# A hybrid decoder layer on one core: sums on DVE, stores from ACT's queue, a bank for the last piece, later turns

## The chip, the cores and the metric

The kernel runs on one core of a Trainium2 chip. The metric is the device time of one launch in microseconds. The core has the tensor engine (TensorE, PE in the profile; its weight loads are PEld), the vector engine (DVE), the scalar engine (ACT), GpSimd (POOL) and SyncE (SP), which here only issues DMAs. Each engine works through its own instructions in order; semaphores hold an instruction until what it reads or overwrites is ready, and everything behind it on that engine waits with it.

## The reference

One layer (DEPTH 1) on 1024 tokens of width 1024, float32. A token mixer (sliding-window attention with sinks beside a gated DeltaNet, merged by gates, one output projection `mixed`), then a squared-ReLU MLP, both post-norm with adaLN modulation:

```
x  = layer_norm(ALPHA * x + (1 + gt1) * mixed, ln1_g, ln1_b)
u2 = x * (1 + sc2) + sh2
h  = square(relu(u2 @ w_ff1 + b_ff1))                  # 1024 x 4096
x  = layer_norm(ALPHA * x + (1 + gt2) * (h @ w_ff2 + b_ff2), ln2_g, ln2_b)
```

The change lies wholly behind the mixer's projections: in `mixed` (the product with `w_out`) and the first layer norm, in FF1 (`u2 @ w_ff1`) and in FF2 (`h @ w_ff2`).

## The kernel before

**Precision.** Each float32 operand is split into a high and a low part (`split_s`: ACT copies the high part, DVE subtracts to give the low one some matmuls later), and each product is three matmuls: high x high, high x low, low x high.

**Order of the work.** The order on TensorE, DVE and ACT is written out by hand. `count[0]` counts the matmuls issued; `at(p, f, ...)` puts a piece of work at matmul number p, `after(n, ...)` n matmuls from now, and before each matmul the loop emits what is due (`run_events`). The number of an event is a place in the engines' program order, not a time: an engine that is late does the work later, in that order. SP and POOL are not held to it; their order is made by a planner with a model of costs, and then is as fixed as the others'.

**The mix stage (from E0 to F0).** Four stretches s of the product with w_out, over token tiles t of 128. When a tile's second half is there, `mix_done` gates it, adds the residual, takes bn statistics, has ACT take a square root (L1392) and DVE normalise (`norm`, L1394 to L1397), and stores the tile. `u2_done` then plans the tile's turn: TensorE transposes it (`u2_turn`, L1407, into PSUM tag b, two buffers), ACT copies it out with scale and bias (L1410), and it is split into U11, U21, U22 and the sums T1 to T4. Tiles 6 and 7 come last.

**FF1 (from F0 to G0).** A Strassen-like scheme: the 1024 x 4096 product is cut in block pairs i = 0 to 15, and each pair is seven products m of 12 matmuls (L1866), 84 in all. For i below EARLY = 5 the products 1 and 2 of all pairs come first, and the rest follow in periods of 60 matmuls; from i = 5 a pair is 84 in a row. `PROD` says which weights a product takes: a and g are the first weight tile before and after sums, b the second after a sum, d their difference x. So each pair needs four additions on 128 x 512 (`f_sums`: x and the second tile; `f_sums2`: the first tile), after its two weight tiles are loaded (`f_load`, tile fraw, two pairs deep) and ahead of the splits `f_beta`, `f_gamma`, `f_delta`. x is in one buffer. For i = 1 and i of 5 and more the sums are on DVE, for i = 2, 3 and 4 on POOL.

ACT copies the result of a begun bank out with its bias (`part`, L1585), which frees the bank for the next product that adds into it; `full` adds a second product on DVE and `square` does relu and square; `last_block` does the same for the last product; `block_done` stores a finished block (c = 0, 2, 3) to the DRAM tensor hf_d with `put`, on SP's queue. `again` reads one block back, `h_sums` and `h_sums2` form and store the sums of blocks that FF2 takes.

Meanwhile POOL makes FF2's weight sums: `t_load` loads a pair of w_ff2 tiles (wx), `t_make` does four subtractions and stores them to wt_d. The first 13 of 16 rounds fall in FF1.

**FF2 (from G0).** Seven products m in the order 1, 2, 6, 5, 3, 7, 4, each of eight steps s of 24 matmuls over four PSUM banks (L1907). `s_load` loads a step's two operands, `s_split` splits operand j = 0 and 1; the first steps are placed from p15, the start of pair 15. In the last product the last four steps are done tile by tile, and the last tile in two pieces of 256 columns, both in its one bank; `gated` adds each piece up, `norm2` does the second layer norm and stores it.

The line numbers are those of the profile: L1407 and L1410 are in `u2_turn`, L1435 in `sub`, L1543 in `add_`, L215 and L216 in `split_s`.

Of the kernel before, what the change touches and what calls it, by code (L numbers as in the profile page):

```python
# [9 lines left out]
F32 = mybir.dt.float32  # L10
F32R = mybir.dt.float32r
BF16 = mybir.dt.bfloat16
AF = mybir.ActivationFunctionType
ALU = mybir.AluOpType
# [3 lines left out]
P = 128  # L18
D = 1024
S = 1024  # L20
KT = D // P
NT = S // P
HALF = 512
# [11 lines left out]
def hybrid_layer_kernel(ctx: ExitStack, tc: tile.TileContext,  # L35
                        x, c, w_ada, b_ada, w_in, conv_w, a_log, dt_bias, sinks, dn_norm_w,
                        w_oa, w_ob, w_out, ln1_g, ln1_b, w_ff1, b_ff1, w_ff2, b_ff2,
                        ln2_g, ln2_b, out, dbg=None):
    nc = tc.nc
    x, c, out = x[0], c[0], out[0]  # L40
# [6 lines left out]
    V, A, G, T = nc.vector, nc.scalar, nc.gpsimd, nc.tensor  # L47

    const = ctx.enter_context(tc.tile_pool(name="const", bufs=1))
    wp = ctx.enter_context(tc.tile_pool(name="wp", bufs=4))  # L50
# [4 lines left out]
    def psum(tag, bufs, name=None):  # L55
        return ps.tile([P, HALF], F32, tag=tag, bufs=bufs, name=name or tag)
# [23 lines left out]
    hf_d = dram.tile([7, D_FF // (2 * P), P, HALF], F32, name="hf_d")  # L80
# [21 lines left out]
    eps_ln = const.tile([P, 1], F32, name="eps_ln")  # L102
# [92 lines left out]
    events, count, order = [], [0], [0]  # L195

    def at(p, f, *args):
        order[0] += 1
        heapq.heappush(events, (p, order[0], f, args))

    def after(n, f, *args):
        at(count[0] + n, f, *args)
# [275 lines left out]
    for step in ('t0 s0 o00 o01 w0 w1 d4 t1 s1 v203 o10 v235 o11 v256 m0 t2 p2 s2 v304 o20 v346 o21 m1 t3 p3 s3 v404 o30 v446 o31 m2 '  # L478
                 't4 p4 s4 v504 o40 v546 o41 m3 t5 p5 s5 r0 v604 o50 v646 o51 m4 t6 p6 s6 v704 o60 v746 o61 m5 t7 p7 s7 o70 o71 m6').split():
        f, k = step[0], int(step[1])  # L480
# [900 lines left out]
    def mix_done(second, q, t, pt):  # L1381
        r = rs[t]
        rq = r[:, halves[q]]
        tm = pe.tile([P, HALF], F32, tag="t", name="tm", bufs=6)
        V.tensor_tensor(out=tm, in0=pt, in1=gt1[:, halves[q]], op=ALU.mult)
        V.scalar_tensor_tensor(out=rq, in0=rq, scalar=ALPHA, in1=tm, op0=ALU.mult, op1=ALU.add)
        V.bn_stats(out=parts[:, t, q, :], in_=rq)
        if not second:
            return
        st = pe.tile([P, 4], F32, tag="st", name="st", bufs=3)  # L1390
        V.bn_aggr(out=st[:, 0:2], in_=parts[:, t].rearrange("p q s -> p (q s)"))
        after(1, lambda: A.activation(out=st[:, 2:3], in_=st[:, 1:2], func=AF.Sqrt, bias=eps_ln))  # L1392

        def norm():  # L1394
            V.reciprocal(out=st[:, 3:4], in_=st[:, 2:3])
            V.tensor_scalar(out=r, in0=r, scalar1=st[:, 0:1], scalar2=st[:, 3:4], op0=ALU.subtract, op1=ALU.mult)
            nc.gpsimd.dma_start(out=res_d[t], in_=r)  # L1397
        after(4, norm)

    def u2_turn(j, us, ks):  # L1400

# [72 lines left out]
    wt, bank = [], 0  # L1474
# [28 lines left out]
    for s in range(4):  # L1503
        q, t0 = (0, 1, 1, 0)[s], 4 * (s // 2)
        if s != 2:
            del wt[:]
        groups = [[0, 1], [2, 3]] if s < 2 else [[4, 5], [6, 7]] if s == 2 else [[4, 5], [6], [7]]
        for ts in groups:
            pts = []
            for t in ts:  # L1510
                tag = ("mm", "a", "mm", "c", "mm", "a")[bank % 6]
                bank += 1
                pts.append(psum(tag, {"mm": 3, "a": 2, "c": 1}[tag]))
            for c in range(4):
                if len(wt) == c:
                    run_events(count[0])
                    wt.append(ready.pop(0))
                for pt, t in zip(pts, ts):
                    mix_mm(pt, slice(t * P, (t + 1) * P), c)
            for pt, t in zip(pts, ts):  # L1520
                at(max(count[0] + (14 if s == 2 and t > 5 else 1), E0 + 28), mix_done, s % 2 == 1, q, t, pt)
                if s % 2 == 1:
                    at(count[0] + 1, u2_done, t, count[0] + (26 if t == 7 else 34))

# [15 lines left out]
    def add_(E, out, a, b):  # L1542
        E.tensor_tensor(out=out, in0=a, in1=b, op=ALU.add)  # L1543
# [33 lines left out]
        f = i + NPAIR * (c // 2)  # L1577
        return bf1[:, f:f + 1]

    def put(m, i, t):  # L1580
        nc.sync.dma_start(out=hf_d[m - 1, i], in_=t)

    def part(i, c, pt):

# [1 line left out]

    def block_done(i, c):
        if c != 1:
            put({0: 1, 2: 2, 3: 4}[c], i, tls[i, c])

    def square(i, c):
        t = tls[i, c]
# [58 lines left out]
    for i in range(1, NPAIR):  # L1651
        if i < EARLY:
            b = pos[i, 5]
            E = V if i == 1 else G
            at(b - 70, f_load, i)
            at(b - (26 if i == 1 else 46), f_sums, i, E)
            at(b - (25 if i == 1 else 44), f_sums2, i, E)
            at(b - 17, f_beta, i)
            at(b - 3, f_gamma, i)
            at(b + 10, f_delta, i)  # L1660
        else:
            b = pos[i, 1]
            at(b - 104, f_load, i)
            at(b - (34 if i == EARLY else 76), f_alpha, i)
            at(b - (28 if i == EARLY else 66), f_sums, i, V)
            at(b - (27 if i == EARLY else 60), f_sums2, i, V)
            at(b + (8 if i == EARLY else -44), f_gamma, i)
            at(b + (26 if i == EARLY else -9), f_beta, i)
            at(max(b - (0 if i == EARLY else 22), pos[i - 1, 7] + 13), f_delta, i)
# [155 lines left out]
    for s in range(7 * NS):  # L1825
        p = G0 + 24 * s
        at((p15 + 14, p15 + 26, p15 + 62, p15 + 64)[s] if s < 4 else p - 96 - 28, s_load, s)
        for j in range(2):
            if s < 2:
                q = p15 + (40, 64)[s] + 8 * j  # L1830
            elif s >= 6 * NS:
                q = p - (94 if s > 6 * NS else 70) + 10 * j
            else:
                q = p - 46 + 10 * j
            at(q, s_split, s, j)
# [52 lines left out]
    def take(dst, pt, copy):  # L1888
        if copy:
            A.activation(out=dst, in_=pt, func=AF.Copy)  # L1890
        else:
            add_(V, dst, dst, pt)

    for n, m in enumerate(ORDER):
        ab = "C" if m in (2, 5, 3) else "A"
        begin = m in (1, 2, 5)
# [2 lines left out]
                         for tag in (("mm", "mm", "a", "c") if ab == "A" else ("mm", "a", "b", "b"))]  # L1899
        bank = chain[ab]  # L1900

        def step(s, f, t, lo=0, up=HALF):
            for x_ in range(3):
                run_events(count[0])
                (ah_, al_), (bh, bl) = stp[s, 0], stp[s, 1]
                a, b = ((ah_, bh), (ah_, bl), (al_, bh))[x_]
                T.matmul(bank[t][:, lo:up], lhsT=a[:, f, t * P:(t + 1) * P], rhs=b[:, f, lo:up],  # L1907
                         start=begin and s % NS == 0 and f == 0 and x_ == 0,
                         stop=s % NS == NS - 1 and f == 1 and x_ == 2, skip_group_check=True)
                count[0] += 1  # L1910

        def steps(ss, tile_first):
            if tile_first:
# [15 lines left out]
        if m == 4:  # L1929
            for _ in steps(range(s0 + 1, s0 + NS - LAST), False):  # L1930
                pass
            for t in range(4):

                cuts = [0, HALF] if t < 3 else [0, HALF // 2, HALF]
                for i, (lo, up) in enumerate(zip(cuts, cuts[1:])):
                    for s in range(s0 + NS - LAST, s0 + NS):
                        for f in range(2):
                            step(s, f, t, lo, up)
                    after(1, gated, 4 + t, lo, up, 1 + i, bank[t][:, lo:up])
                after(1, norm2, 4 + t, [(HALF, D), (0, HALF)], 1 + len(cuts) - 1)  # L1940
            break
        for _ in steps(range(s0 + 1, s0 + NS - 1), False):
# [43 lines left out]
```

## Time and profile before

| what | us |
|---|---|
| runs: median, lowest, highest of 3 | 1913.79, 1913.71, 1917.88 |
| profiled execution: time | 1912.24 |
| its span | 1910.5 |
| TensorE busy in the span | 1833.2 |
| DVE busy | 1289.8 |
| ACT busy | 976.0 |
| POOL busy | 422.6 |

The profile is of one execution. Times in it count from the span's start. A group of instructions is written "line engine operation out<-in", with the idle time of the engine before it and what ended that idle time in brackets. In the list of waits the three numbers are the total, the number of waits and the longest. In the stretches of time the columns are, for each engine, busy time and number of instructions, then the granted clock of TensorE, the share of time in which the DMA engines were busy, and GB/s. A matmul of 128 x 512 is shown as about 0.39 us long while one starts each 0.227 us, since matmuls overlap. The letter behind PE is the PSUM tag that it writes.

### The profile page before, as it was taken

What the parts mean: (1) busy time and instruction counts of PE and PEld (TensorE: products, weight loads), DVE (VectorE), ACT (ScalarE), POOL (GpSimd) and SP (SyncE); (2) the same over time, 40 slices, a digit from 0 to 9 for tenths busy, and PEclk for the clock granted to TensorE, in tenths of its full rate; (3) what the DMA queues carried; (4) which work ended last, traced back from release to release, by engine and by line L of the source; (5) the groups of instructions that cost most, each with busy time, mean ns of one, the idle gap of its engine ahead of it and who ended that gap; (6) DMA issues with size and microseconds to landing.
All of it is one profiled execution on the core that took longest, in us unless ns stands there. A gap on an engine that the chain in (4) does not pass through costs nothing.

```text
span 1910.5 us, 26004 instructions
## 1 busy us (share of the span) xinstructions
PE 1833.2 (96%) x9137; PEld 1513.2 (79%) x9137; DVE 1289.8 (68%) x2395; ACT 976.0 (51%) x2105; POOL 422.6 (22%) x521
## 2 busy tenths in 40 slices
PE   7999999999999999999999999995899999999997
PEld 5977788788887878888888888774687887888886
DVE  7678598998856666666644446872677556676696
ACT  3689666666654445544634223562454554434441
POOL 7333233443331000000001100035644002300000
PEclk7999999999999999999999999997999999999998
DMA  9655632232257444554337444465888449955571
GB/s 257 181 189 198 209 95 82 59 97 79 72 195 218 149 137 144 156 152 142 112 132 264 141 136 154 144 230 201 287 274 279 143 153 394 362 192 176 198 243 44
DMA packets 261644, 337.72 MB, mean 177 GB/s; under 512 B 25237, under 2 KB 170342, under 8 KB 261258
## 3 DMA queue, kind: packets, MB, share of 16 engines
q1 hardware_dynamic: 230954, 227.62, 37.7%
q0 software_dynamic: 30560, 108.44, 16.6%
q8 instruction: 72, 1.18, 0.2%
q14 instruction: 58, 0.48, 0.1%
HBM read 231.40 MB, written 102.51 MB: 175 GB/s over the span
## 4 chain that ended last, share of the span: by engine, by line
PE 73%; DVE 10%; DMA 4%; ACT 4%; issue 3%; POOL 2%; SPq 0%; POOLq 0%; ACTq 0%; DVEq 0%
PE mm L248 32%; PE mm L1907 6%; PE mm L1866 5%; PE a L1907 4%; PE b L1907 3%; PE b L1866 3%; PE c L1907 2%; DVE wl L216 2%; PE c L909 2%; PE a L1866 1%; DMA wx<-in_w_ff_dram 1%; PE mm L1498 1%; POOL wx L1435 1%; PE mm L188 1%; PE mm L187 1%
## 5 line engine op out<-in xcount | busy, mean ns | idle before, releaser
L248 PE MATMUL mm<-uh,wl 128*128 128x512 f32 x800 | 331.4, 414 | 0.0
L248 PE MATMUL mm<-ul,wh 128*128 128x512 f32 x800 | 320.8, 401 | 0.0
L248 PE MATMUL mm<-uh,wh 128*128 128x512 f32 x800 | 317.3, 397 | 0.0
L216 DVE TENSOR_TENSOR sp<-sraw,sp 128x1024 fp32r<-128x1024 f32 x112 | 137.8, 1264 | 75.3 <-ACT sp L215 75.3
L215 ACT ACTIVATE sp<-sraw 128x1024 fp32r<-128x1024 f32 x112 | 112.7, 1053 | 125.0 <-PE b L1907 65.4
L248 PEld LDWEIGHTS mm<-ul,wh 128*128 128x128 f32 x800 | 150.6, 188 | 26.5 <-issue 0.2
L248 PEld LDWEIGHTS mm<-uh,wl 128*128 128x128 f32 x800 | 151.4, 189 | 22.8 <-issue 3.9
L248 PEld LDWEIGHTS mm<-uh,wh 128*128 128x128 f32 x800 | 151.3, 189 | 21.2 <-issue 0.2
L1907 PE MATMUL mm<-sp 128*128 128x512 f32 x528 | 136.1, 389 | 0.0
L216 DVE TENSOR_TENSOR wl<-fraw,wh 128x1024 fp32r<-128x1024 f32 x43 | 62.4, 1453 | 80.6 <-ACT wh L215 80.3
L1907 PEld LDWEIGHTS mm<-sp 128*128 128x128 f32 x528 | 99.1, 188 | 20.5
L1435 POOL TENSOR_TENSOR wx<-wx 128x512 f32<-128x512 f32 x64 | 94.9, 1482 | 75.3 <-DMA wx<-in_w_ff_dram 73.8
L216 DVE TENSOR_TENSOR wl<-wr,wh 128x1024 fp32r<-128x1024 f32 x81 | 98.7, 1219 | 8.1 <-ACT wh L215 8.1
L215 ACT ACTIVATE wh<-wr 128x1024 fp32r<-128x1024 f32 x81 | 84.9, 1049 | 21.6 <-PE c L1498 12.3
L1907 PE MATMUL a<-sp 128*128 128x512 f32 x336 | 92.6, 389 | 0.0
L1169 ACT ACTIVATE vn<-a,brk 128x128 f32<-128x128 f32 x64 | 23.5, 367 | 108.1 <-PE a L1167 107.2
L1593 ACT ACTIVATE t<-t 128x512 f32<-128x512 f32 x48 | 30.1, 627 | 93.1 <-DVE t L1543 93.1
L853 POOL TENSOR_TENSOR sm<-sm 128x256 f32<-128x256 f32 x56 | 55.6, 993 | 97.7 <-ACT sm L849 65.0
L842 DVE CUSTOM_DVE_ANT_0 nscore<-a,amask,nsink 128x256 f32<-128x256 f32 (+1 forms) x128 | 54.6, 464 | 33.5 <-PE a L835 32.7
L1907 PEld LDWEIGHTS a<-sp 128*128 128x128 f32 x336 | 63.1, 188 | 13.1
L1907 PE MATMUL b<-sp 128*128 128x512 f32 x288 | 72.8, 389 | 0.0
L215 ACT ACTIVATE wh<-fraw 128x1024 fp32r<-128x1024 f32 x43 | 45.2, 1053 | 40.7 <-POOL fraw L1543 33.3
(520 smaller groups left out, 4746.9 us busy)
## 6 DMA issues: line engine op xcount, KB each, us to landing
wr<-in_w_in_dram SPq DMA_DIRECT2D x60, 512.0 KB, 3.6
sraw<-hf_d SPq DMA_DIRECT2D x56, 512.0 KB, 4.4
fraw<-in_w_ff_dram SPq DMA_DIRECT2D x32, 512.0 KB, 4.5
hf_d<-t SPq DMA_DIRECT2D x64, 256.0 KB, 4.5
wx<-in_w_ff_dram POOLq DMA_DIRECT2D x32, 512.0 KB, 6.4
wt_d<-wx POOLq DMA_DIRECT2D x32, 512.0 KB, 3.7
sraw<-wt_d SPq DMA_DIRECT2D x32, 512.0 KB, 4.6
sraw<-in_w_ff_dram SPq DMA_DIRECT2D x24, 512.0 KB, 5.7
```

The lines of the kernel that those rows point to most:

```text
L187: T.matmul(t, lhsT=wh[:, k, :], rhs=xl[k][:, sl], start=False, stop=False)
L215: A.activation(out=hi, in_=src, func=AF.Copy)
L216: after(lag, lambda: V.tensor_tensor(out=lo, in0=src, in1=hi.bitcast(F32), op=ALU.subtract))
L248: T.matmul(ts[half], lhsT=w[:, k, :], rhs=xx[k][:, sl], start=k == 0 and m == 0, stop=k == KT - 1 and m == 2)
L842: V.tensor_tensor_reduce(out=ns[:, i, 1:1 + W], in0=sc[:, i * 2 * P:i * 2 * P + W], in1=amask[:, mo:mo + W], scale=-1.0, scalar=nsink[:, 2 ...
L853: G.tensor_tensor(out=sm[:, :, 1 + P:1 + 2 * P], in0=sm[:, :, 1:1 + P], in1=sm[:, :, 1 + P:1 + 2 * P], op=ALU.add)
L909: T.matmul(av[:, 0:256], lhsT=vt[:, b, :], rhs=p_[:, m, :], start=p_ is full and m == 0, stop=p_ is prods[-1][1] and m == 1)
L1169: after(1, lambda: A.activation(out=vn, in_=Wp[:, 0:P], func=AF.Copy, scale=brk[:, n, h:h + 1]))
L1435: E.tensor_tensor(out=out, in0=a, in1=b, op=ALU.subtract)
L1593: A.activation(out=t, in_=t, func=AF.Relu)
L1866: T.matmul(pt, lhsT=a[:, k0 + k, :], rhs=b[k], start=begin and k == 0 and x_ == 0, stop=k == 3 and x_ == 2, skip_group_check=True)
L1907: T.matmul(bank[t][:, lo:up], lhsT=a[:, f, t * P:(t + 1) * P], rhs=b[:, f, lo:up], start=begin and s % NS == 0 and f == 0 and x_ == 0, sto ...
```

## The change

- The sums of i = 2, 3, 4 go from POOL to DVE, at 40 and 36 matmuls ahead of product 5 instead of 46 and 44.
- `block_done` stores the finished blocks from ACT's queue. The other users of `put` stay on SP.
- For tiles 6 and 7 the square root comes 20 and 12 matmuls after `mix_done` instead of 1, the normalisation three behind it, and the turn at 46 and 40 matmuls instead of 34 and 26.
- The splits of FF2's first two steps come at 52 and 76 matmuls after p15 instead of 40 and 64.
- In FF2's last product the last tile's columns 256 to 511 go to a bank of their own (`tail`, PSUM tag b). All its steps are then in two pieces, and what earlier products had left in the old bank for these columns is added by a new function, `cut_gate`, from the copy that DVE has of it. Matmuls of the second piece do not advance the count.

```diff
         V.bn_aggr(out=st[:, 0:2], in_=parts[:, t].rearrange("p q s -> p (q s)"))
-        after(1, lambda: A.activation(out=st[:, 2:3], in_=st[:, 1:2], func=AF.Sqrt, bias=eps_ln))
+        lag = {6: 20, 7: 12}.get(t, 1)
+        after(lag, lambda: A.activation(out=st[:, 2:3], in_=st[:, 1:2], func=AF.Sqrt, bias=eps_ln))
...
-        after(4, norm)
+        after(lag + 3, norm)
...
-                    at(count[0] + 1, u2_done, t, count[0] + (26 if t == 7 else 34))
+                    at(count[0] + 1, u2_done, t, count[0] + {6: 46, 7: 40}.get(t, 34))
...
-    def put(m, i, t):
-        nc.sync.dma_start(out=hf_d[m - 1, i], in_=t)
+    def put(m, i, t, q=None):
+        (q or nc.sync).dma_start(out=hf_d[m - 1, i], in_=t)
...
-            put({0: 1, 2: 2, 3: 4}[c], i, tls[i, c])
+            put({0: 1, 2: 2, 3: 4}[c], i, tls[i, c], A)
...
-            E = V if i == 1 else G
             at(b - 70, f_load, i)
-            at(b - (26 if i == 1 else 46), f_sums, i, E)
-            at(b - (25 if i == 1 else 44), f_sums2, i, E)
+            at(b - (26 if i == 1 else 40), f_sums, i, V)
+            at(b - (25 if i == 1 else 36), f_sums2, i, V)
...
-                q = p15 + (40, 64)[s] + 8 * j
+                q = p15 + (52, 76)[s] + 8 * j
...
+    CUT, tail = HALF // 2, []
+
+    def cut_gate(t):
+
+        tm = wp.tile([P, D], F32, tag="wr", name="tm", bufs=2)[:, 0:HALF - CUT]
+        V.tensor_tensor(out=tm, in0=acc[t][:, CUT:HALF], in1=rows_["gt2"][:, CUT:HALF], op=ALU.mult)
+        add_(V, rr[t][:, CUT:HALF], rr[t][:, CUT:HALF], tm)
+    at(G0 + 6 * PS + 77, cut_gate, NT - 1)
...
+        if m == 4:
+            tail.append(psum("b", 2))
+
         def step(s, f, t, lo=0, up=HALF):
+            if m == 4 and t == 3 and up - lo == HALF:
+                step(s, f, t, 0, CUT)
+                step(s, f, t, CUT, HALF)
+                return
+            own = up - lo < HALF and lo > 0
+            to = (tail[0] if own else bank[t])[:, lo:up]
...
-                T.matmul(bank[t][:, lo:up], lhsT=a[:, f, t * P:(t + 1) * P], rhs=b[:, f, lo:up],
-                         start=begin and s % NS == 0 and f == 0 and x_ == 0,
+                T.matmul(to, lhsT=a[:, f, t * P:(t + 1) * P], rhs=b[:, f, lo:up],
+                         start=(begin or own) and s % NS == 0 and f == 0 and x_ == 0,
                          stop=s % NS == NS - 1 and f == 1 and x_ == 2, skip_group_check=True)
-                count[0] += 1
+                count[0] += lo == 0
...
-                    after(1, gated, 4 + t, lo, up, 1 + i, bank[t][:, lo:up])
+                    after(1, gated, 4 + t, lo, up, 1 + i, (tail[0] if i else bank[t])[:, lo:up])
```

More of the change, by code (lines that the diff above doesn't have):

```diff
@@ L1932, in hybrid_layer_kernel @@
             for t in range(4):
-                cuts = [0, HALF] if t < 3 else [0, HALF // 2, HALF]
+                cuts = [0, HALF] if t < 3 else [0, CUT, HALF]
                 for i, (lo, up) in enumerate(zip(cuts, cuts[1:])):
```

## The prediction, made before the change was run

> **What bounds the kernel now.** I read the engine table and the slices first, then who TensorE waited for, then the order of time at each wait.
>
> ```profile
> span 1910.5 us, 26004 instructions
> PE 1833.2 (96%) x9137; PEld 1513.2 (79%) x9137; DVE 1289.8 (68%) x2395; ACT 976.0 (51%) x2105; POOL 422.6 (22%) x521
> PE   7999999999999999999999999995899999999997
> ```
>
> TensorE is busy for 96% of the span, so only a stretch in which it waits or runs slow can give time back. The slices show one (the 28th, half busy: 1290 to 1337 us, early in FF1) and the two ends. Four parts of the change touch the waits after 1225 us:
>
> ```profile
> PE a L1866 <- ACT wh L215: 13.4, 2, 10.6
> PE c L1866 <- ACT wh L215: 9.4, 2, 9.1
> ...
> PE mm L1866 <- ACT t L1585: 4.0, 2, 2.2
> PE b L1407 <- ACT rawu L1410: 3.9, 2, 3.7
> PE c L1907 <- DVE acc L1803: 3.8, 1, 3.8
> PE b L1866 <- ACT t L1585: 3.4, 1, 3.4
> ```
>
> **The early FF1 sums: the largest term.** Block pairs i = 2, 3, 4 form their weight sums on POOL (f_sums, f_sums2: four instructions), behind t_make, which shares POOL's in-order queue.
>
> ```profile
> 1296.67 1.26 POOL L1435 TENSOR_TENSOR wx<-wx 128x512 f32<-128x512 f32 x1 [6.27 <-DMA wx<-in_w_ff_dram]
> 1297.89 1.25 POOL L1435 TENSOR_TENSOR x<-fraw 128x512 f32<-128x512 f32 x1
> ...
> 1306.26 1.28 POOL L1435 TENSOR_TENSOR fraw<-fraw 128x512 f32<-128x512 f32 x1
> 1301.62 1.06 ACT L215 ACTIVATE wh<-fraw 128x1024 fp32r<-128x1024 f32 x1 [14.21 <-POOL fraw L1543]
> 1302.72 0.80 PE L1866 MATMUL a<-mh,wh 128*128 128x512 f32 x1 [10.61 <-ACT wh L215]
> 1366.74 0.39 PE L1866 MATMUL mm<-u11h,wh 128*128 128x512 f32 x1
> 1436.17 2.72 PE mm L1866 x12
> ```
>
> The first sum sits behind a t_make that waited for its load, and the four span 1297.89 to 1307.5 us, a t_make step between each two. ACT's split of the first summed tile waits for it (14.21 us), and TensorE's product 5 of i = 2 waits for ACT (10.61). TensorE was ready at 1302.72 - 10.61 = 1292.1; by product 1 of i = 5, at 1366.74, it had issued 180 matmuls (three periods of 60), at 2.72/12 = 0.227 us 40.8 us of work. It took 74.6: 33.8 us are lost, waits and slow matmuls behind them (0.80 us long where 0.39 is usual).
>
> On DVE, where i = 1 has its sums already, one takes 0.69 us:
>
> ```profile
> 1272.87 0.69 DVE L1435 TENSOR_TENSOR x<-fraw 128x512 f32<-128x512 f32 x1
> ...
> 1286.19 0.68 DVE L216 TENSOR_TENSOR wd<-x,wd 128x512 fp32r<-128x512 f32 x1
> ...
> 1302.70 1.23 DVE L216 TENSOR_TENSOR wl<-fraw,wh 128x1024 fp32r<-128x1024 f32 x1 [15.24 <-ACT wh L215]
> 1267.07 2.61 SPq L1539 DMA_DIRECT2D fraw<-in_w_ff_dram  x2
> DMA to landing us min/median/max: 4.0/4.6/6.5
> ```
>
> The weights of i = 2 were issued by 1269.7 and landed within 6.5 us, by 1276. The one x tile is free when DVE has subtracted wd of i = 1, at 1286.9; DVE then does one block sum (sb) and stands idle for 15.24 us. With the sums in that gap: four sums 1286.9 to 1289.7, the half that ACT needs (the first two) ready at 1288.3, split on ACT 1.06 and on DVE, behind sb (0.7), 1.23: 1291.6, against TensorE at 1292.1. So i = 2 no longer waits, by half a microsecond. For i = 3 and 4 the question is whether DVE fits into a period at full pace, 60 x 0.227 = 13.6 us. By the means of FF1 as a whole:
>
> ```profile
> L216 DVE TENSOR_TENSOR wl<-fraw,wh 128x1024 fp32r<-128x1024 f32 x43 | 62.4, 1453 | 80.6 <-ACT wh L215 80.3
> L1435 DVE TENSOR_TENSOR sa<-t 128x512 f32<-128x512 f32 x31 | 26.8, 863 | 0.7 <-ACT t L1594 0.2
> L1435 DVE TENSOR_TENSOR fraw<-fraw 128x512 f32<-128x512 f32 x26 | 20.1, 774 | 0.8
> ```
>
> Two wl 2.9, wd 0.7, four sums 3.1, two adds of the same shape as wd 1.4, four block sums (sa, t, sa, sb) at 0.86, 3.4: 11.5 us, 85% of the period. It fits, with 2 us to spare; these means hold what DVE lost to POOL's steps in FF1. I take back 29 of the 33.8: about 1.2 us per period stay, and 1 for slow matmuls. Bounds: all 33.8, or 18 if DVE becomes the bound (33.8 less the 15.6 of the first rival).
>
> What else hangs on the DVE at these places: the sums now stand behind delta's subtraction (they share x) and ahead of sb and the next wl; late is then wl, and TensorE with it. The step from 46 to 40 matmuls ahead costs 1.4 us of lead, counted in the above.
>
> **Stores from ACT's queue.** 48 stores of finished blocks (c = 0, 2, 3) leave SP. The trace has no store on ACT. Nearest rows:
>
> ```profile
> 1309.85 0.32 SPq L1581 DMA_DIRECT2D hf_d<-t  x1
> 1268.49 0.58 POOL L1698 DMA_DIRECT2D wt_d<-wx  x1 [0.30 <-POOL wx L1435]
> hf_d<-t SPq DMA_DIRECT2D x64, 256.0 KB, 4.5
> ```
>
> An issue takes 0.32 us on SP; POOL waits 0.30 for its own result first; so 0.62 each on ACT. Below: 0.32 and the wait overlapped. Above: 4.5, if ACT were held until the transfer lands. I take 0.62, since SP and POOL issue without waiting for landings: three per later period of 84 matmuls (19.0 us) make 1.9 us on an engine that is busy 57% of the time (the column after DVE's):
>
> ```profile
> 1500.00:1550.00 50.00, 50.00 (x222) 41.45 (x221) 30.57 (x40) 28.26 (x41) 0.00 (x0) 1.00 0.38 130
> ```
>
> Behind a store in ACT's order stand the bias copies (part) and splits that TensorE needs. It counts where ACT is already late, at the two 'mm <- ACT t' waits: 2 x 0.6 = +1.2. SP's loads no longer stand behind those stores, but no wait of TensorE above ends on a late load or store of theirs: 0. The other stores (a21, sa, sb) and the reload stay on SP.
>
> **The turns of tiles 6 and 7.**
>
> ```profile
> 1227.25 0.29 ACT L1392 ACTIVATE st<-st,eps_ln 128x1 f32<-128x1 f32 x1 [3.80 <-DVE st L1391]
> 1231.93 1.09 PE L1407 MATMUL b<-ident,r 128*128 128x128 f32 x8 [3.70 <-ACT rawu L1410]
> 1233.33 0.63 PE L1498 MATMUL c<-wh,mh 128*128 128x512 f32 x1
> ```
>
> Tile 6's square root stands in ACT's order ahead of two weight splits and eight bias copies, and idles it 3.80 us; TensorE waits 3.70 for those copies, then runs about eight matmuls at 0.43 us for 0.227 (+1.6). With the root 19 matmuls later, the first split moves into the idle time, but the copies can only start when the transposes are there (1226), and eight copies and a split take 4 us: TensorE still waits about 2 us. Gain 1.7 + 1.6 = 3.3. Against it: tile 6's normalisation on DVE comes 19 matmuls later, just ahead of tile 7's mix, and tile 7's turn 14 matmuls (3.2 us) later, while TensorE already waits 0.3 us for a split at product 5 of i = 0 (the shorter of the two waits of c for ACT above, 9.4 - 9.1). I take 2.5. Bounds: 5.3 back, or 2 us lost at product 5 of i = 0.
>
> **The first splits of FF2**, moved 12 matmuls later:
>
> ```profile
> 1581.91 1.06 ACT L215 ACTIVATE sp<-sraw 128x1024 fp32r<-128x1024 f32 x1 [1.77 <-DMA sraw<-in_w_ff_dram]
> 1582.87 0.67 ACT L1585 ACTIVATE t<-b,cols 128x512 f32<-128x512 f32 x1
> 1583.59 0.50 PE L1866 MATMUL b<-u22h,wh 128*128 128x512 f32 x1 [3.42 <-ACT t L1585]
> 1590.82 1.52 PE L1907 MATMUL mm<-sp 128*128 128x512 f32 x6
> ```
>
> ACT waits in order for the loads while a bias copy, emitted one matmul later than the second split, stands behind. TensorE loses 3.42, and the last 24 matmuls take 7.23 for 5.44 (+1.8): 5.2. At +52 and +60 both splits come behind that copy (+49), so the wait goes. Late next: the second split, done on DVE by about 1584.2, against FF2's first matmul at 1590.82 - 5.2 = 1585.6. I take 4.8 (0 to 5.2).
>
> **The last piece.** Product 4, tile 7 gets bank b for columns 256 to 511.
>
> ```profile
> 1889.80 3.17 PEld L1907 LDWEIGHTS c<-sp 128*128 128x128 f32 x25
> 1902.27 0.43 DVE L1803 TENSOR_TENSOR acc<-c,gt 128x256 f32<-128x256 f32 x1 [4.45 <-PE c L1907]
> 1879.34 0.69 DVE L1803 TENSOR_TENSOR acc<-mm,gt 128x512 f32<-128x512 f32 x1 [6.74 <-PE mm L1907]
> ```
>
> DVE works from 1879.34 to 1897.8 (1902.27 - 4.45) with nothing but short waits for the square root; TensorE's second piece waits 3.78 us for DVE's read of the first (the row c <- DVE acc above). With its own bank it ends near 1889.80 + 2 x 3.17 = 1896.1, before DVE wants it: DVE's 4.45 us idle goes. Costs: 24 matmuls of the product's first four steps become 48 of half width, at 3.17/25 = 0.127 us 6.1 for 5.4: +0.6 (0 if they ran at half of 0.227). cut_gate, two operations of 0.43, lies in DVE's 6.74 us of idle time before 1879.34; without that cover 0.9. Net 3.9 (2.9 to 4.5).
>
> **Sum.** 29 - 1.2 + 2.5 + 4.8 + 3.9 = 39.0 us from the profiled execution's 1912.24 (span 1910.5 and 1.7 around it): 1873.2. The median of the runs shown, 1913.79, lies 1.55 above it: **1874.8**, and I say 1874.5.
>
> **Rivals.**
> *DVE becomes the bound of early FF1* (1885). For: a block sum beside a POOL step takes 1.77 us instead of 0.69:
>
> ```profile
> 1280.95 1.77 DVE L1435 TENSOR_TENSOR sa<-t 128x512 f32<-128x512 f32 x1
> ```
>
> If all four sums and three block sums of a period are slowed by 1.08 so, DVE needs 11.5 + about 6 = 17.5 us for 13.6: 3.9 lost in each of three periods and in i = 5, 15.6 instead of the 5 allowed, 1885. Against: the means above hold such meetings already, and are 0.77 and 0.86. The Trainium skill (SBUF — State Buffer, "SBUF: two separate sides") says that a DVE instruction with two SBUF inputs and a GpSimd instruction that reads SBUF lock each other out for the whole instruction. By that rule the moved sums, which have two inputs, are worse neighbours of t_make than on POOL's own queue; the 1.77 agrees with it. Taken for every sum and block sum it gives the 1885, the means give the 1874.5.
>
> *The weights land late* (1883). At full pace the loads are asked for in shorter order. If one takes 11.4 us, not 4.6, as a load at the end of FF1 did:
>
> ```profile
> 1570.46 11.42 DMA sraw<-in_w_ff_dram
> ```
>
> it comes 4.6 us behind the 6.8 (30 matmuls) between load and sums: 13.8 over three periods instead of 5. Against: 6.5 at most in this stretch.
>
> *Only the sums do what is said* (1884): the late turns come back as a wait at product 5 (+2), the splits' wait moves to FF2's first matmul (0 gained): 2.5 + 2 + 4.8 = 9.3 lost of the sum.
>
> *Slower: ACT held by its stores* (1949). If a store kept ACT until landing (4.5 us), three per 19.0 us beside 57% of work (10.8) are 24.3: +5.3 in 11 periods, and 2 x 4.5 + 7.7 = 16.7 for 13.6 in five: +3.1; 74 us on 1875. It decides, against a period, once a store costs ACT over 2.7 us. Against: SP's 0.32.
>
> **Chances.** Forecast 0.58 (its own range 1866 to 1880), DVE bound 0.18, late loads 0.10, sums only 0.09, ACT held 0.05. The range, 1863 to 1889, runs from the upper bounds of the gains (33.8 + 5.3 + 5.2 + 4.5 = 48.8: 1865, and the 'mm <- ACT t' waits eased by 2 as well) to DVE bound with one more term missing. A change of under 0.3% (5.7 us) can't be told from none; every case but the last gains over 20: faster 0.94, same 0.01, slower 0.05.
>
> **What would show it.** Right: TensorE's waits for 'wh' between 1285 and 1340 under 2 us each, no 'acc L1803' wait, no 'b <- ACT t' wait at FF1's end, and product 1 of i = 5 about 45 us behind the moment at which TensorE was ready for product 5 of i = 2, instead of 74.6. Wrong: DVE busy over 95% there with TensorE waiting for 'wl' or 'wh' (first rival); sums ending idle on a DMA (second); stores on ACT longer than 1 us each (last); TensorE waiting longer at product 5 of i = 0 (turns).

## The result, and the profile after

The changed kernel takes 1883.46 us (median of 4 runs, 1882.44 to 1885.78) against 1913.75 (1912.53 to 1917.88) for the kernel before on the same chip: a ratio of 0.984 (95% interval 0.9822 to 0.9857), 30.3 us faster. The forecast was 1874.5. The sign and the whole range (1863 to 1889) held, but the time lies outside the forecast's own range (1866 to 1880): the sum of 39.0 us was 8.7 too high.

The head of the profile page after, engine rows and TensorE's slices:

```profile
span 1880.3 us, 26014 instructions
...
PE 1827.3 (97%) x9161; PEld 1509.4 (80%) x9161; DVE 1309.7 (70%) x2409; ACT 978.0 (52%) x2105; POOL 411.7 (22%) x509
...
PE   7999999999999999999999999999899999999997
```

The half-busy slice of before is gone. Who TensorE waited for between 1200 and 1890 us (total, times, longest):

```profile
PE mm L1866 <- ACT t L1586: 5.3, 3, 2.7
PE a L1866 <- DVE u21l L216: 2.2, 1, 2.2
PE mm L1866 <- DVE wl L216: 2.1, 1, 2.1
PE b L1408 <- ACT rawu L1411: 2.0, 1, 2.0
PE c L1866 <- DVE wl L216: 2.0, 2, 1.8
```

No wait for wh is left, none of b for ACT's t at FF1's end, and none for acc (L1803): the waits that the change was expected to take away are away. Waits for DVE's wl were there before, in the same stretch of time, though the prediction's list leaves them out:

```profile
PE b L1866 <- DVE wl L216: 1.5, 1, 1.5
PE c L1866 <- DVE wl L216: 1.1, 2, 0.6
PE a L1866 <- DVE wl L216: 1.1, 1, 1.1
```

They were 3.7 us in all and are 4.5 now (with 0.4 of a, not shown). The wait of mm for ACT's bias copies has grown from 4.0 to 5.3 us, and the wait for u21l is new.

Where the time went is read from the starts of a few matmuls: F0 (FF1's first), product 5 of i = 2, product 1 of i = 5, of i = 6 and of i = 15, and G0 (FF2's first). In the timeline of after they are:

```profile
1233.27 0.39 PE L1866 MATMUL mm<-u11h,wh 128*128 128x512 f32 x1
...
1291.65 0.39 PE L1866 MATMUL a<-mh,wh 128*128 128x512 f32 x1
...
1337.16 0.39 PE L1866 MATMUL mm<-u11h,wh 128*128 128x512 f32 x1
...
1368.43 0.39 PE L1866 MATMUL mm<-u11h,wh 128*128 128x512 f32 x1
...
1544.93 0.39 PE L1866 MATMUL mm<-u11h,wh 128*128 128x512 f32 x1
...
1563.97 1.30 PE L1926 MATMUL mm<-sp 128*128 128x512 f32 x5
```

and in that of before, where the prediction has not shown them (product 1 of i = 6 and of i = 15):

```profile
1392.49 0.39 PE L1866 MATMUL mm<-u11h,wh 128*128 128x512 f32 x1
...
1566.41 0.39 PE L1866 MATMUL mm<-u11h,wh 128*128 128x512 f32 x1
```

The same starts in the profiled execution of every kernel that ran give this table (us). E0 is the first matmul of the mix stage. Ahead of E0, where nothing is changed, executions differ by up to 12 us (E0 lies between 1137.5 and 1150), so the column from E0 to the end compares kernels better than one execution's total. "Full pace" is the number of matmuls by 0.2267 us.

| kernel | E0 to F0 | F0 to i=2, m=5 | to i=5, m=1 | to i=15, m=1 | to G0 | G0 to end | E0 to end |
|---|---|---|---|---|---|---|---|
| full pace | | | 40.8 | 193.2 | 19.0 | | |
| before | 98.4 | 66.8 | 64.0 | 199.7 | 24.4 | 319.7 | 773.0 |
| after | 95.5 | 58.4 | 45.5 | 207.8 | 19.0 | 316.3 | 742.5 |
| after, run again | 95.7 | 59.7 | 45.0 | 206.0 | 19.4 | 316.3 | 742.1 |
| sums alone | 99.6 | 56.0 | 44.4 | 204.6 | 25.6 | 319.6 | 749.8 |
| stores on SP | 95.5 | 56.5 | 47.2 | 204.8 | 19.3 | 316.5 | 739.7 |
| turns old | 99.9 | 57.8 | 44.2 | 208.7 | 19.4 | 316.2 | 746.2 |
| no FF2 weight sums | 95.5 | 59.9 | 40.8 | 194.7 | 19.1 | 316.3 | 726.3 |
| norm 6 later | 95.5 | 59.2 | 47.0 | 203.6 | 21.2 | 315.8 | 742.3 |
| held | 95.5 | 59.9 | 40.8 | 204.8 | 19.0 | 325.8 | 745.8 |
| held, norm 6, SP | 95.5 | 56.9 | 40.8 | 201.0 | 19.0 | 322.6 | 735.8 |
| held, 11 rounds, SP | 95.5 | 57.7 | 40.8 | 202.6 | 19.0 | 316.3 | 732.0 |
| held, 11 rounds | 96.8 | 57.2 | 40.8 | 203.6 | 19.0 | 316.4 | 733.8 |

Every stage of after gained what was forecast or nearly so, but one: the pairs from i = 5 to 15, which no part but the stores touches, take 8.1 us longer (207.8 against 199.7). Most of that is i = 5 itself: from its product 1 to that of i = 6 it took 1392.49 - 1366.74 = 25.75 us before and takes 31.27 after, for 96 matmuls, 21.8 us at full pace. There the timeline after has these rows among others (start, duration, engine, line, operation, and the idle time before it with its releaser in brackets):

```profile
1344.73 2.97 POOL L1436 TENSOR_TENSOR wx<-wx 128x512 f32<-128x512 f32 x2 [0.53 <-DMA wx<-in_w_ff_dram]
...
1344.78 1.78 DVE L1436 TENSOR_TENSOR sa<-t 128x512 f32<-128x512 f32 x1
1346.49 4.52 DVE L216 TENSOR_TENSOR wl<-fraw,wh 128x1024 fp32r<-128x1024 f32 x2
1348.84 0.50 PE L1866 MATMUL mm<-mh,wl 128*128 128x512 f32 x1 [2.12 <-DVE wl L216]
...
1355.32 0.68 DVE L1544 TENSOR_TENSOR t<-t,a 128x512 f32<-128x512 f32 x1
1356.04 0.63 ACT L1594 ACTIVATE t<-t 128x512 f32<-128x512 f32 x1 [7.44 <-DVE t L1544]
1356.70 0.63 ACT L1595 ACTIVATE t<-t 128x512 f32<-128x512 f32 x1
1357.36 0.33 ACTq L1582 DMA_DIRECT2D hf_d<-t  x1
1357.78 0.69 ACT L1586 ACTIVATE t<-mm,cols 128x512 f32<-128x512 f32 x1 [0.46 <-ACT t L1595]
1358.53 0.50 PE L1866 MATMUL mm<-mh,wd 128*128 128x512 f32 x1 [2.43 <-ACT t L1586]
```

Beside POOL's subtractions DVE's block sum takes 1.78 us, and two wl subtractions 4.52, where one takes 1.23 in the prediction's rows. This stretching is not what is new: in i = 5 of the kernel before the same two took as long.

```profile
1372.70 4.54 DVE L216 TENSOR_TENSOR wl<-fraw,wh 128x1024 fp32r<-128x1024 f32 x2
```

But there they began 6.0 us behind product 1 of i = 5 (1366.74), and in after 9.3 us behind it (1337.16): DVE is 3.4 us later against TensorE. TensorE waits 2.12 for the wl. DVE works back to back from 1341.8 until 1356.0; ACT sits idle 7.44 us for DVE's last addition, and its two steps of the square and the store stand in ACT's order ahead of the bias copy that TensorE then waits 2.43 us for. Not all of the loss is waiting. The stretch of i = 5, columns as in the prediction's windows, for before:

```profile
1366.70:1392.50 25.80, 22.45 (x98) 17.89 (x98) 20.25 (x19) 14.58 (x22) 14.21 (x13) 1.00 0.81 284
```

and for after:

```profile
1337.20:1368.40 31.20, 26.08 (x97) 19.82 (x96) 22.42 (x25) 15.25 (x22) 16.20 (x16) 0.89 0.78 261
```

TensorE is idle for 3.4 us of it before (25.80 - 22.45) and for 5.1 after (31.20 - 26.08). That is 1.8 of the 5.4 us by which the stretch is longer; the other 3.6 are matmuls that run slow, at a granted clock of 0.89 instead of 1.00.

Two theories come out of the rows. **Theory A**: DVE has no slack once it carries the sums, because POOL's steps of t_make stretch its instructions; it comes late out of i = 4. **Theory B**: the stores hold up ACT's bias copies.

### The profile page after: what moved, and what is told of

Read it like the earlier page. It is cut to its first block, busy times and chain, and to the rows that moved or that the text cites. A ratio compares the mean times of both kernels' runs of the same rounds, so it can differ in the third digit from the quotient of the medians.

```text
span 1880.3 us, 26014 instructions
## 1 busy us (share of the span) xinstructions
PE 1827.3 (97%) x9161; PEld 1509.4 (80%) x9161; DVE 1309.7 (70%) x2409; ACT 978.0 (52%) x2105; POOL 411.7 (22%) x509
## 4 chain that ended last, share of the span: by engine, by line
PE 75%; DVE 11%; ACT 5%; issue 3%; DMA 2%; POOL 0%; ACTq 0%; SPq 0%; DVEq 0%; POOLq 0%
PE mm L248 33%; PE mm L1926 6%; PE mm L1866 6%; PE b L1926 4%; PE a L1926 4%; PE b L1866 3%; PE mm L1499 2%; DVE wl L216 2%; PE c L1926 2%; PE c L909 2%; PE a L1499 1%; PE a L1866 1%; PE mm L188 1%; PE mm L187 1%; PE mm L186 1%
## 5 line engine op out<-in xcount | busy, mean ns | idle before, releaser
L248 PEld LDWEIGHTS mm<-uh,wh 128*128 128x128 f32 x800 | 151.2, 189 | 21.2 <-issue 0.2
L1436 POOL TENSOR_TENSOR wx<-wx 128x512 f32<-128x512 f32 x64 | 100.3, 1567 | 77.4 <-DMA wx<-in_w_ff_dram 75.7
L1926 PE MATMUL b<-sp 128*128 128x512 f32 (+1 forms) x336 | 80.0, 374 | 0.0
L1926 PEld LDWEIGHTS b<-sp 128*128 128x128 f32 x336 | 60.5, 188 | 11.2
```

The costliest lines, as they stand in the source:

```text
L248: T.matmul(ts[half], lhsT=w[:, k, :], rhs=xx[k][:, sl], start=k == 0 and m == 0, stop=k == KT - 1 and m == 2)
L1436: E.tensor_tensor(out=out, in0=a, in1=b, op=ALU.subtract)
L1926: T.matmul(to, lhsT=a[:, f, t * P:(t + 1) * P], rhs=b[:, f, lo:up], start=(begin or own) and s % NS == 0 and f == 0 and x_ == 0, stop=s % ...
```

## The experiments

### The sums alone, and the stores back on SP

The kernel before with only this part of the change (its L1653 to L1657):

```
-            E = V if i == 1 else G
-            at(b - (26 if i == 1 else 46), f_sums, i, E)
-            at(b - (25 if i == 1 else 44), f_sums2, i, E)
+            at(b - (26 if i == 1 else 40), f_sums, i, V)
+            at(b - (25 if i == 1 else 36), f_sums2, i, V)
```

> The kernel before, with the sums of i = 2, 3, 4 on DVE and nothing else changed. In the changed kernel the stretch from product 1 of i = 5 to product 1 of i = 15 (852 matmuls, 193.2 us at 0.2268) took 207.8 us, in the kernel before 199.7: 8.1 us lost again behind the 29.1 gained in i = 2 to 4. Theory A (DVE has no slack left once it carries the sums, and POOL's t_make steps stretch it): the late stretch is as long here, 205 to 210 us, and the time is 1913.8 - 29 + 8 = about 1893 us. Theory B (the stores on ACT hold up the bias copies that TensorE waits for): the late stretch stays at 199 to 201, and the time is about 1885 us.

The changed kernel with

```
-            put({0: 1, 2: 2, 3: 4}[c], i, tls[i, c], A)
+            put({0: 1, 2: 2, 3: 4}[c], i, tls[i, c])
```

> The changed kernel with the 48 stores back on SP's queue. Theory A: the late stretch (product 1 of i = 5 to product 1 of i = 15) stays at 205 us or more and the time within 3 us of the changed kernel's 1883.5. Theory B: the late stretch falls to 201 us or less and the time to about 1876 us.

**Measured.** The sums alone: 1896.28 us (1887.58 to 1901.9), ratio 0.9892 (0.9862 to 0.9923). Stores on SP: 1883.42 (1881.86 to 1884.79), ratio 0.9829 (0.9814 to 0.9844), not to be told from the changed kernel.

TensorE's waits with the sums alone:

```profile
PE b L1865 <- DVE wl L216: 2.8, 1, 2.8
PE c L1865 <- DVE wl L216: 1.7, 2, 1.1
PE a L1865 <- DVE wl L216: 1.4, 1, 1.4
PE mm L1865 <- DVE wl L216: 1.0, 1, 1.0
```

**What follows.** With no store on ACT TensorE already waits 6.9 us for DVE's wl, 3.7 in the kernel before, and i = 5 to 15 take 204.6 us: 4.9 of the 8.1 us come with the sums. Of these, 3.4 are in i = 5 (29.1 us against 25.75), where the program is that of the kernel before and POOL begins eight subtractions in both. DVE comes to it later: the same two wl begin 8.3 us behind product 1 of i = 5, not 6.0. The loss there is mostly waiting: TensorE is idle for 6.2 us of the stretch (29.10 - 22.95), and the granted clock is 1.00.

```profile
1350.00:1379.10 29.10, 22.95 (x97) 17.70 (x96) 22.29 (x25) 14.92 (x22) 15.96 (x16) 1.00 0.78 266
```

Early FF1 (F0 to i = 5) gains 30.4 us by the sums alone, the forecast's 29. Theory B cannot carry the shortfall: the stores on SP give back 3.0 us in this stretch of one execution, and nothing that the median shows. Part of it may be theirs.

### No weight sums for FF2

The changed kernel with the subtractions of t_make left out; the rounds still load and store. So what FF2 reads as its weight sums are the plain weights.

```
-        sub(G, b11, b12, b11)
-        sub(G, b12, b22, b12)
-        sub(G, b22, b22, b11)
-        sub(G, b21, b21, b22)
```

> The changed kernel without the four subtractions of t_make on POOL (left out: FF2's weight sums; its loads and stores stay, so FF2 multiplies other numbers). Theory A with POOL's steps as the cause: DVE's operations of 128 x 512 in FF1 go back to 0.69 us each (mean now 0.77 and more), the late stretch falls to 196 us or less, the time to about 1872 us. Theory A without them (DVE is simply full): the late stretch stays over 203 us. Theory B: unchanged, 1883 us.

**Measured.** 1869.99 us (1867.67 to 1870.26), ratio 0.976 (0.9743 to 0.9776). The stretch of 45 us that ends at product 1 of i = 5, columns as in the prediction's windows, for before:

```profile
1321.70:1366.70 45.00, 33.67 (x120) 26.13 (x121) 24.41 (x24) 16.68 (x24) 32.14 (x31) 0.77 0.70 245
```

for after:

```profile
1292.20:1337.20 45.00, 42.81 (x180) 34.54 (x180) 39.14 (x37) 22.61 (x33) 25.29 (x24) 0.96 0.91 321
```

and without POOL's subtractions:

```profile
1290.90:1335.90 45.00, 45.00 (x201) 37.25 (x200) 30.55 (x41) 23.55 (x35) 6.95 (x13) 1.00 1.03 369
```

DVE's groups of 1292 to 1385 us (busy us, mean ns), after:

```profile
L216 DVE TENSOR_TENSOR wl<-fraw,wh 128x1024 fp32r<-128x1024 f32 x14 | 21.3, 1524 | 12.6 <-ACT wh L215 12.6
...
L216 DVE TENSOR_TENSOR wd<-x,wd 128x512 fp32r<-128x512 f32 x6 | 8.6, 1426 | 1.3 <-ACT wd L215 1.3
...
L1436 DVE TENSOR_TENSOR x<-fraw 128x512 f32<-128x512 f32 x5 | 6.5, 1294 | 0.1
```

and without POOL's subtractions:

```profile
L216 DVE TENSOR_TENSOR wl<-fraw,wh 128x1024 fp32r<-128x1024 f32 x16 | 19.6, 1224 | 16.6 <-ACT wh L215 16.4
...
L1436 DVE TENSOR_TENSOR x<-fraw 128x512 f32<-128x512 f32 x6 | 4.1, 687 | 0.1
L216 DVE TENSOR_TENSOR wd<-x,wd 128x512 fp32r<-128x512 f32 x6 | 4.1, 686 | 1.0 <-ACT wd L215 1.0
```

**What follows.** DVE, the column after PEld's, is busy for 54% of the stretch before (24.41 of 45), 87% after (39.14) and 68% without POOL's subtractions (30.55), with more instructions done (41 against 37). The subtraction that makes x or the low part of wd (128 x 512) takes 0.69 us without POOL's and 1.3 to 1.4 on average with them. With them gone, i = 2 to 4 run at full pace (40.8 us) with the loads and the stores as before, and i = 5 to 15 at 194.7, 1.5 above full pace. This is theory A: POOL's subtractions, by what they do to DVE, cost 4.7 us in i = 2 to 4 and 13 in the rest of FF1. Of these 13, 5.0 were there before (199.7 against 194.7); the other 8.1 are what the change adds. It also speaks against late loads: TensorE at full pace asked for them no later. The Trainium skill (SBUF — State Buffer, "SBUF: two separate sides") calls it a lock held for a whole instruction, against a GpSimd instruction that reads SBUF; the trace agrees, 0.69 us beside idle POOL and up to 1.78 beside a busy one.

### The old turns, and the changed kernel again

The changed kernel with the square root, normalisation and turn of tiles 6 and 7 where they were:

```
-        lag = {6: 20, 7: 12}.get(t, 1)
+        lag = 1
-                    at(count[0] + 1, u2_done, t, count[0] + {6: 46, 7: 40}.get(t, 34))
+                    at(count[0] + 1, u2_done, t, count[0] + (26 if t == 7 else 34))
```

> The changed kernel with the square roots and turns of tiles 6 and 7 at their old places. By the two traces the later turns gave 2.6 us up to FF1's start and cost 2.2 of it again by product 5 of i = 2 (a wait of 2.2 us for u21's low part at product 2 of i = 0): so about 1884 us, the wait of TensorE for the bias copies (b) back at 3.7 us and the one for u21l gone. If the later turns are worth the 2.5 us that I predicted, 1886 us; if they are worth the 2.6 and the u21l wait has another cause, the u21l wait stays.

The changed kernel as it is, in the same group:

> The changed kernel once more, as the yardstick of this group: 1883 us, within 4 us by chip.

**Measured.** Old turns: 1889.06 us (1883.58 to 1890.49), ratio 0.9853 (0.9836 to 0.9871). The changed kernel again: 1886.17 (1885.52 to 1888.46), ratio 0.9842 (0.9828 to 0.9856). The intervals overlap; the medians lie 2.9 us apart.

**What follows.** From E0 to F0 the new turns are 4.2 to 4.4 us shorter, and from there to product 5 of i = 2 they are 0.6 to 1.9 longer, which leaves 2.3 to 3.8; over E0 to the end it is 3.6 to 4.1 us. That is the forecast's 2.5 and a little more, in the profiled executions; the medians alone don't show it. With the old turns TensorE waits 3.9 us for the bias copies and not at all for u21l, so the wait for u21l comes from the later turns, as expected. The two executions of the changed kernel differ by at most 1.8 us in any one stage: the table's noise.

### Tile 6's normalisation later

TensorE waits 2.2 us for u21l, DVE's split of the turned tiles. Here tile 6's normalisation comes 6 matmuls later, behind what DVE does for the first pairs:

```
-        after(lag + 3, norm)
+        after(lag + (9 if t == 6 else 3), norm)
```

> The changed kernel with tile 6's normalisation six matmuls later than the change has it (nine behind its square root instead of three), so that DVE adds up tile 7 and subtracts u21's low part before it waits for that root. If the 2.2 us wait of TensorE for u21l (product 2 of i = 0) comes from DVE's 1.76 us wait for the root in ACT's order, the wait goes, and the stretch from FF1's start to product 5 of i = 2 falls from 58.4 to 55 to 56 us; the time from the changed kernel's by about 2.5 us. If DVE is simply full there, the wait only moves to a later product and the stretch stays at 58.

**Measured.** 1890.63 us (1884.43 to 1894.88), ratio 0.9863 (0.9842 to 0.9885). TensorE's waits from 1225 to 1300 us:

```profile
PE b L1408 <- ACT rawu L1411: 3.8, 2, 2.0
...
PE a L1866 <- DVE u21l L216: 0.4, 1, 0.4
```

**What follows.** The wait for u21l falls from 2.2 to 0.4, and a second one of 1.8 us, for ACT's copies, takes its place; F0 to product 5 of i = 2 stays at 59.2 us. There is no gain: of the two cases expected it is the second, the wait moves.

### POOL's rounds held back

POOL is not held to the matmul count: it runs a step as soon as its inputs are there. So it is given something to wait for: DVE writes one column of the first two load tiles, from which their loads must wait, and the rounds are planned from product 5 of i = 5:

```
+            if n == 0:
+                V.memset(ts[j][:, 0:1], 0.0)
...
-        p = pos[EARLY, 1] - 60 + T_STEP * n if n < T_IN else G0 + 60 + T_STEP * (n - T_IN)
+        p = pos[EARLY, 5] + T_STEP * n if n < T_IN else G0 + 60 + T_STEP * (n - T_IN)
```

> The changed kernel with t_make's 13 rounds of FF1 held back: DVE writes one column of the first two wx tiles at product 5 of i = 5, and the first load waits for that. Nothing is left out. Theory A with POOL's steps as the cause: without them the three periods from product 5 of i = 2 to product 1 of i = 5 take 41 us (45.5 in the changed kernel, 40.8 of pure work), i = 5 loses under 2 us instead of 9, and later pairs lose somewhat more, since the rounds now reach to FF1's end; the late stretch 198 to 204 us instead of 207.8; the time 8 to 12 us under the changed kernel's. If DVE is full without them, neither stretch changes. Against it: the loads of FF2's first steps and of the rows fall together with the last rounds, and FF2's first matmuls could wait (up to 5 us).

The same with tile 6's normalisation later and the stores on SP:

> The changed kernel with t_make held back as in hold, tile 6's normalisation as in norm6, and the stores back on SP's queue. If the three are separate (about 10, 2.5 and 3 us of FF1), FF1 takes about 315 us instead of 330.7, and the time is about 15 us under the changed kernel's, near 1868. If the stores on ACT cost only where POOL's steps have already made ACT late, their 3 us are in the 10 already: near 1871.

**Measured.** Held: 1890.06 us (1887.89 to 1896.4), ratio 0.9868 (0.9848 to 0.9888), no faster than the changed kernel. With the two other edits: 1878.15 (1876.6 to 1883.15), ratio 0.9805 (0.9787 to 0.9823). In the first, TensorE's longest wait from 1500 to 1620 us, around G0:

```profile
PE mm L1928 <- ACT sp L215: 6.4, 1, 6.4
```

the wait of ACT behind it:

```profile
ACT sp L215 <- DMA sraw<-hf_d: 12.4, 1, 12.4
```

and, in POOL's timeline, the last store of the rounds and the first of six row loads behind it:

```profile
1555.29 0.58 POOL L1700 DMA_DIRECT2D wt_d<-wx  x1 [0.30 <-POOL wx L1436]
1555.86 0.54 POOL L1342 DMA_DIRECT2D gt<-gt_d  x1
```

**What follows.** The held rounds do what theory A says: 40.8 us for i = 2 to 4, at full pace with the sums on DVE, and i = 5 loses 1.6 us (1359.46 - 1336.12 = 23.34, 21.8 at full pace) instead of 9.5. But the last of 13 rounds now ends at 1555.9, 4 us ahead of FF2, whose loads of the first blocks keep ACT idle for 12.4 us; FF2 takes 325.8 us instead of 316.3. The gain is given back at the next stage, and the 8 to 12 us expected did not come. With the two other edits FF2 still takes 322.6, 6.3 more than in the changed kernel, and the time misses both values expected, 1868 and 1871, by 10 and 7 us.

### Eleven held rounds instead of thirteen

The held kernel with five rounds in FF2 instead of three, once with the stores on SP and once on ACT:

```
-    T_IN, T_STEP = 13, 72
+    T_IN, T_STEP = 11, 72
```

> The changed kernel with the steps of t_make held back to product 5 of block pair i = 5 (a DVE write of one column into the first two load tiles, from which their loads wait), 11 of its rounds in FF1 instead of 13 (the other five in FF2), and the stores back on SP. In the run with 13 held rounds and the turn of tile 6 moved, FF2's first product still lost about 6 us (322.56 us from FF2's first matmul to the end, 316.3 in the changed kernel), because the last rounds, the row loads and FF2's first loads met. If that meeting is the cause, 11 rounds end near 1525 us, some 40 us ahead of FF2: FF2 takes 316.5 again. Theory A (DVE has no slack once POOL's steps lock it out): from product 5 of i = 2 to product 1 of i = 5 40.8 us again, from there to product 1 of i = 15 about 200, and from the first mix matmul to the end about 729 us (742.3 in the changed kernel): 12 to 13 us faster than the changed kernel. If the meeting has nothing to do with the rounds, FF2 stays at 322 and the gain at 6. Theory B (the stores on ACT are what the shortfall is made of) expects no more than the 3 us that stores on SP alone gave: about 739.

> The same with the stores on ACT, as in the changed kernel. Without POOL's steps in early FF1, DVE has 30% of its time free there, and ACT's two DMA issues and waits per period find cover: if the stores' 3 us are a cost only beside a full DVE, the stretch from product 1 of i = 0 to product 1 of i = 15 is the same as with SP's stores, within 1 us. If a store costs ACT's own time wherever it stands, it is 3 us longer. Theory A: 40.8 us from product 5 of i = 2 to product 1 of i = 5 in both.

**Measured.** With SP: 1872.95 us (1869.86 to 1874.05), ratio 0.9768 (0.9747 to 0.9789). With ACT: 1878.35 (1872.13 to 1881.09), ratio 0.9802 (0.978 to 0.9824). With SP, the stretch up to product 1 of i = 5:

```profile
1289.00:1334.00 45.00, 45.00 (x201) 37.24 (x200) 30.45 (x41) 24.06 (x35) 0.00 (x0) 1.00 0.60 204
```

**What follows.** FF2 is back at 316.3 and 316.4 us, so the loss at FF2's start was the rounds' doing: held and held with 11 rounds (both with the stores on ACT) differ in this one number of the program, and FF2 takes 325.8 and 316.4. Which of the transfers that met there was the one in the way was not taken apart. The version with SP is faster than both the kernel before (by 2.3%) and the changed one (its interval lies wholly below the changed kernel's). DVE does in it what it does without POOL's subtractions: 30.45 us of 45, 41 instructions. From i = 5 on it takes 202.6, not the 200 expected: the rounds, now wholly there, still cost 9 us above full pace.

On the stores the two agree within 0.5 us from F0 to i = 15 (301.1 and 301.6), as expected if they cost only beside a full DVE. But their medians lie 5.4 us apart, with intervals that just touch, and from i = 5 to 15 each kernel with the stores on ACT is longer than its counterpart on SP, by 1.0 to 3.0 (203.6 and 202.6; 207.8 or 206.0 and 204.8). A cost of 1 to 3 us is likely, but two executions of one kernel differ by 1.8 in this stretch; it isn't settled.

## Why the prediction was right, and where it was not

- **The early sums, 29 us.** From TensorE's readiness for product 5 of i = 2 to product 1 of i = 5, 74.6 us were to become 45: 45.5 in after, 44.4 with the sums alone. No wait for wh is left, as said. The argument from DVE's idle gap held.
- **"It fits, with 2 us to spare"** is the step that failed. The forecast put 13 DVE instructions into a period at 11.5 us, a mean of 0.88, and the period at full pace is 13.6. In after the 37 instructions in the stretch took 39.14 us, a mean of 1.06, and 13 of these need 13.8 us: DVE does not fit, the more so as it still stands idle for 5.9 of the 45 us. Without POOL's subtractions the mean is 0.75, and 13 need 9.7. That DVE's share was forecast at 85% and measured at 87% is luck, since the periods themselves had become longer. The terms that were too small are the subtraction for wd, put at 0.7 as if POOL never met it and 1.43 on average in the rows of after, and the sums, put at 0.77 each, of which x took 1.29. The means of "FF1 as a whole" did not hold enough of POOL: in the kernel before its subtractions in FF1 end at 1472.7 us, and a third of FF1 lies behind that.
- **What stands behind the moved sums was not costed.** DVE goes into i = 5 with its work late by 3.4 us, and the loss appears there, as waits and as slow matmuls behind them. i = 5 to 15 lost 8.1 us against before; about 5 of them come with the sums alone.
- **The signs.** All four that were named for being right came: no wait for wh, none for acc, none of b at FF1's end, and 45.5 us for 45. DVE over 95% busy, the sign of the first rival, did not. None of them looked at i = 5, so they could not tell that 8.7 us would be missing.
- **DVE becomes the bound (the first rival, 1885).** Its time is nearer than the forecast's, 1883.46 against 1885, and its mechanism is the one shown. Its place was not, so the nearness is in part luck. It put 15.6 us into i = 2 to 5 together, 3.9 in each. These lost 4.7 above full pace in i = 2 to 4 and 9.5 in i = 5, 14.2, and the kernel before had 4.0 of the 9.5 already.
- **Stores, +1.2 us.** An issue behind ACT's own result takes 0.33 us and 0.40 to 0.46 of waiting: the row above has the next instruction 0.42 us behind the start of the store, less than the 0.62 taken. The sum counted them at two places; the runs make 1 to 3 us in late FF1 likely and do not settle it.
- **Turns, 2.5 us.** 3.6 to 4.1 by the kernel without them, 2.3 to 3.8 up to product 5 of i = 2. TensorE still waits 2.0 us for the copies, as forecast. The loss that was feared at product 5 of i = 0 came at product 2: 2.2 us for u21l.
- **The first splits, 4.8 us.** Product 1 of i = 15 to G0 went from 24.4 to 19.0, full pace: 5.4, just above the upper bound of 5.2. FF2's first matmul waits for no split.
- **The last piece, 3.9 us.** G0 to the end went from 319.7 to 316.3: 3.4. In the timeline of DVE in the tail the wait of 6.10 us ahead of the last tiles is still there (6.74 before), but the last tile's two pieces wait for TensorE no more:

```profile
1853.70 0.69 DVE L1803 TENSOR_TENSOR acc<-mm,gt 128x512 f32<-128x512 f32 x1 [6.10 <-PE mm L1926]
...
1870.84 0.42 DVE L1803 TENSOR_TENSOR acc<-c,gt 128x256 f32<-128x256 f32 x1
...
1872.09 0.41 DVE L1803 TENSOR_TENSOR acc<-b,gt 128x256 f32<-128x256 f32 x1
```

- **Late loads and the held ACT** fell: TensorE ran at full pace over the same loads without POOL's subtractions, and a store takes ACT 0.33 us, not 4.5.

Against the kernel before, the profiled executions from E0 to the end are 30.5 us apart. By stages: 2.9 in the mix stage, 27.0 in early FF1, -8.1 in i = 5 to 15, 5.4 at FF1's end and 3.4 in FF2 (the last digit by rounding). Of the 39.0 forecast, 8.5 are missing, and all but 1.6 of these in i = 5 to 15, where only the stores' 1.2 had been put.

## What to carry to other kernels

When work moves onto an engine and takes away its waits, cost the stage behind as well: those waits were where the engine caught up, and a stretch that "fits" with little to spare hands its lateness on. Take the means of its instructions from a stretch in which the other engines do what they will do there. If another engine lengthens its instructions (POOL here: 39.1 us of DVE work for 37 instructions, where 30.5 do for 41 without it), move that engine's work out of the full stretch, by giving it something to wait for, and look where the moved work ends: thirteen rounds gave all of it back at FF2's first loads, eleven did not.

## What the runs showed of the hardware that was not expected

- The stretching of DVE by POOL goes on through a group: two wl in a row took 4.52 us beside POOL's subtractions, in both kernels, where one takes 1.22 on average without them. POOL pays too: two of its subtractions took 2.97 us in the row above, where one in the prediction's rows takes 1.26.
- DVE's additions that read one input from PSUM were not stretched. In FF1 of after the 14 additions t<-t,mm took 0.68 to 0.69 us each, also the four that overlapped a subtraction of POOL by more than 0.3 us; the 16 subtractions for wd, with both inputs in SBUF, took up to 1.82.
- DMA traffic did not stand in the way: without POOL's subtractions TensorE kept full pace and a granted clock of 1.00 with a DMA share of 1.03 and 369 GB/s, more than in any other stretch shown here.
- What a wait of TensorE costs is not told by its length. In the kernel with 11 held rounds and the stores on ACT, two waits at the first matmul of product 7 of a pair:

```profile
1428.51 0.50 PE L1868 MATMUL mm<-mh,wd 128*128 128x512 f32 x1 [2.86 <-ACT t L1586]
...
1508.04 0.50 PE L1868 MATMUL mm<-mh,wd 128*128 128x512 f32 x1 [2.54 <-ACT t L1586]
```

By the starts of the products, the pair of the first (i = 9) lost 3.2 us in all, that of the second (i = 13) 4.5: 1.7 of it in product 7 behind that wait, where nothing waits and the matmuls run slow. Over the two pairs the granted clock is 1.00 and 0.93. Why the shorter wait lowers the clock and the longer one does not, no run here shows.
